# Narrow products padded to the full array, and scan levels issued in three groups, in a two-block transformer kernel

## The chip, the cores and the metric

The kernel runs on one core of a Trainium2 chip, as one program. The metric is the device time of one execution in microseconds (us), the median of three runs. Five engines work in parallel, each through its own list of instructions in order: TensorE (PE, with its weight loads listed as PEld), VectorE (DVE), ScalarE (ACT), GpSimd (POOL) and SyncE (SP), which only starts transfers here. They wait for each other by semaphores.

## The reference

512 tokens of width 1024 pass through two transformer blocks in FP32. The first: half an FFN, a mixed attention (eight heads of block-sparse attention with compressed, selected and window keys, and eight "fox" heads of forgetting attention), half an FFN, a gate. The second: sixteen meta tokens are put ahead, then eight heads of the HGRN2 recurrence beside a convolution, then an FFN with a convolution. What the change touches is, in the reference:

```python
# forgetting attention, a block of 128 queries; c = cumsum(log_f)
logits = (jnp.einsum('bhqd,bhsd->bhqs', qq, k).astype(jnp.float32) * scale
          + cq[..., :, None] - c[:, :, None, :])
p = masked_softmax(logits, kpos[None, :] <= tpos[:, None])
...
# the recurrence S_t = diag(f_t) S_{t-1} + k_t v_t^T, o_t = S_t^T q_t, in chunks
G = jnp.cumsum(gb, axis=-2)
o_inter = jnp.einsum('bhtd,bhdv->bhtv', qb * jnp.exp(G), S)
decay = jnp.exp(jnp.where(causal, G[:, :, :, None, :] - G[:, :, None, :, :], -jnp.inf))
A = jnp.sum(qb[:, :, :, None, :] * kb[:, :, None, :, :] * decay, axis=-1)
o = o_inter + jnp.einsum('bhts,bhsv->bhtv', A, vb)
k_dec = kb * jnp.exp(G[:, :, -1:, :] - G)
S_new = jnp.exp(G[:, :, -1, :])[..., None] * S + jnp.einsum('bhsd,bhsv->bhdv', k_dec, vb)
```

## The kernel before

Activations lie with features on the 128 partitions and tokens along the free dimension. An FP32 product with a weight is three products of rounded parts (`x1h`,`whi`; `x1l`,`whi`; `x1h`,`wlo`, and the same with `x0`): each weight tile `wraw` comes by DMA, ScalarE rounds it to `whi`, VectorE makes the rest `wlo`. Weight projections fill most of TensorE's list; with the two halves of one projection they accumulate in `acc`. Smaller products in plain FP32 run as two passes each, so the trace counts two instructions (`x8` for four products).

The order of the work is written when the program is built. Class `Clocks` keeps a modelled clock for each engine, and `Engine._note` charges each instruction. Small tasks (generators, started with `spawn`) are let in between two weight products by `run` when the planner's clock says that their operands are ready. A task's `yield` is such a place. All instructions are recorded in one helper, so that the profile gives line 144 for all of them and a reader goes by the names of tiles.

Attention. `unit` (L1076) does one head and one block of 128 queries, with 128 to 512 keys. It makes the scores `s` (shown as `b`, a bank of the accumulation memory) from two products of `x1h`/`x1l` parts of q and k. For the fox heads a third product adds the bias: row `extra` of `CC`, which holds the cumulated gates in rows 0 to 7 and their rounding rest in rows 32 to 39, is picked by a column of `selr`, broadcast along the free dimension. Both tiles have 40 rows. Then VectorE takes the minimum, ScalarE the exponential, TensorE transposes `p`, ScalarE copies, TensorE multiplies by `VF`. `ev_aux` (L819) fills `selr` and `CC`.

Recurrence. `hgrn` (L1722) does one of eight heads; while it runs, the main loop goes through the projections of the next. The score matrix of a chunk of 128 tokens is put together from seven levels: at level `hs` the tokens are cut into pairs of blocks of `hs`, `level(hs)` subtracts gates (VectorE), takes exponentials (ScalarE), scales k and q into a tile `wX` (VectorE) and multiplies the two halves. At 64 this is four products of 64 columns, at 32 eight of 32; at 16 to 1, `diag` does 16 of 32 columns for four chunks, and below 16 one of 16x4 for the four last meta tokens, with a mask applied afterwards. The set for the diagonal itself, `diag(5, k, q)`, stands at the start. Each level issues as soon as it is scaled. When all seven are issued, ScalarE copies the blocks of levels 64 and 32 into the matrix `AT`, VectorE masks and sums the small levels (`tmm`, `tm`, `rd`, `am`) and copies `rd` into `AT`, and ScalarE copies the level of 16 in eight pieces. Then TensorE multiplies `am` by `vm` (four queries over the 16 meta tokens) and, per chunk, `AT` by `vt` and the carried state `sv` by `qe`. Squares, `rsqrt`, scaling and transposes (`ident`,`wX`; `ident`,`om`) follow. `carry` (L1912) transposes the decayed keys `kd` and multiplies `kt` by `vt` for three chunks and `km` by `vm` for the meta tokens. `vm` is the fifth part of the tile `vt`, `km` the fourth of `kt`; both have 16 rows, `am` has 16 rows and 4 columns, `om` four rows.

Of the kernel before, what the change touches and what calls it, by code (L numbers as in the profile page):

```python
# [8 lines left out]
FT = mybir.dt.float32  # L9
FR = mybir.dt.float32r  # L10
AF = mybir.ActivationFunctionType
OP = mybir.AluOpType
AX = mybir.AxisListType

SEQ, DM, DFF, META = 512, 1024, 2816, 16
# [3 lines left out]
PRE = 4  # L19
# [6 lines left out]
EPS = 1e-6  # L26
BIG = 1e30
LEVELS = (16, 8, 4, 2, 1)
NS, NZ, NPROB = 10, 3, 8

HALF_GROUPS = {"kk": (768, 1024), "qa0": (0, 128), "cc": (512, 640), "qa1": (256, 384), "vf0": (2328, 2456),
# [260 lines left out]
def build(tc, A, out):  # L292
# [70 lines left out]
    rtok = base.tile([128, 5], FT, name="rtok")  # L363
# [408 lines left out]
    with tc.tile_pool(name="att", bufs=1) as pool:  # L772
# [3 lines left out]
        def kk(name):  # L776
            o, w = KOFF[name]
            return kc[:, o:o + w]

        selr = pool.tile([40, 8], FR, name="selr")  # L780
        CC = pool.tile([40, SEQ], FR, name="CC")
        VF = pool.tile([128, 4, 8, 65], FT, name="VF")
        VS = pool.tile([128, 4, 4, 65], FT, name="VS")
        GF = pool.tile([128, 4, 32], FT, name="GF")
# [33 lines left out]

        def ev_aux(bs):  # L819
            yield lambda: done["rB"]  # L820
            act(selr, kk("sel")[:40], AF.Copy)
            for t in range(4):
                V.tensor_scalar(GF[:, t], bs[t].t[:, 256:288], rtok[:, t:t + 1], None, op0=OP.mult)
                S.activation(VS[:, t, :, 0:64], bs[t].t[:, 0:256].rearrange("p (a d) -> p a d", a=4), AF.Copy,
                             scale=rtok[:, t:t + 1])
                bs[t].free()
                yield
            hs = [sc.get() for _ in range(4)]
            z, e, u, l = (x.t[:8] for x in hs)
            b = yield from banks.take(1)  # L830
            for t in range(4):
                P.transpose(b.t[:8, t * 128:(t + 1) * 128], GF[:, t, 24:32], ident)
            yield
            V.tensor_scalar(z, b.t[:8], pc("b_forget", rows=8), None, op0=OP.add)
            b.free()
            yield

            act(G3, GF[:, :, 0:24], AF.Exp, scale=-1.0)
            S.activation(e, z, AF.Abs)
            act(e, e, AF.Exp, scale=-1.0)  # L840
            yield
            V.tensor_scalar(G3, G3, 1.0, None, op0=OP.add)
            V.reciprocal(G3, G3)
            V.tensor_tensor(G0V, G3.rearrange("p t (h j) -> p t h j", j=3)[:, :, :, 0],
                            kk("vcmp")[:, :, None].to_broadcast([128, 4, 8]), op=OP.mult)

            V.tensor_scalar(u, e, 1.0, None, op0=OP.add)
            yield
            act(l, u, AF.Ln, exact=True)
            V.tensor_scalar(u, u, -1.0, None, op0=OP.add)  # L850
            V.tensor_sub(e, e, u)
            V.tensor_scalar(z, z, 0.0, None, op0=OP.min)
            V.memset(u, 1.0)
            yield
            V.tensor_add(l, l, e)
            V.tensor_sub(z, z, l)
            yield
            V.tensor_tensor_scan(l, u, z, 0.0, op0=OP.mult, op1=OP.add)
            S.activation(CC, causal[:40], AF.Copy, scale=0.0)
            yield  # L860
            S.activation(CC[0:8], l, AF.Copy)
            yield
            V.tensor_sub(CC[32:40], l, CC[0:8].bitcast(FT))
            for x in hs:
                x.free()
            done["aux"] = True
# [212 lines left out]
        def unit(u, hp):  # L1079
            q, k, qt, extra = u["q"], u["k"], u["qt"], u["head"]  # L1080
            n = (qt + 1) * 128
            p = hp.t
            lq = q[:, qt * 128:qt * 128 + 128]
            yield seen(lq, k[0][:, :n], k[1][:, :n])
            s = yield from banks.take(1)
            P.matmul(s.t[:, :n], lq, k[0][:, :n], start=True, stop=False)
            P.matmul(s.t[:, :n], lq, k[1][:, :n], start=False, stop=extra is None)
            if extra is not None:

                P.matmul(s.t[:, :n], selr[:, extra:extra + 1].to_broadcast([40, 128]), CC[:, :n],  # L1090
                         start=False, stop=True)
            for f_ in u["free"]:
                f_()
            yield
            mn = pool.tile([128, 1], FT, name="mn", bufs=8)
            V.tensor_tensor_reduce(out=p[:, :n], in0=s.t[:, :n], in1=causal[:, 512 - n:], scale=1.0,
                                   scalar=3e38, op0=OP.add, op1=OP.min, accum_out=mn)
            s.free()
            yield
            act(p[:, :n], p[:, :n], AF.Exp, scale=-1.0, bias=mn)  # L1100
            yield
            hpt = yield from sc.take()
            t = yield from banks.take(1)
            for kb in range(qt + 1):
                P.transpose(t.t[:, kb * 128:kb * 128 + 128], p[:, kb * 128:kb * 128 + 128], ident)
            hp.free()
            flying["n"] -= 1
            yield
            S.activation(hpt.t[:, :n], t.t[:, :n], AF.Copy)
            t.free()  # L1110
            yield u["ready"]
            o = yield from banks.take(1)
            for kb in range(qt + 1):
                P.matmul(o.t[:, :65], hpt.t[:, kb * 128:kb * 128 + 128], u["v"](kb), start=kb == 0, stop=kb == qt)
            hpt.free()
            yield
            rc = pool.tile([128, 1], FT, name="rc", bufs=8)
            V.reciprocal(rc, o.t[:, 64:65])
            u["fin"](o.t, rc)
            o.free()  # L1120
            u["after"]()
# [454 lines left out]
    with tc.tile_pool(name="hgrn", bufs=1) as pool:  # L1576
# [4 lines left out]
        lb = pool.tile([128, 8], FT, name="lb")  # L1581
        lb1 = pool.tile([128, 8], FT, name="lb1")
        rB2 = pool.tile([128, TC], FT, name="rB2")
        ATs = []
        for i in range(2):
            t = pool.tile([128, 4, 128], FT, name=f"AT{i}")
# [6 lines left out]
        for n_, c_ in (("q", 2), ("f", 1), ("i", 1), ("g", 2), ("a", 1), ("gb", 1), ("cv", 1), ("yb", 2), ("k", 1),  # L1593
                       ("G", 1), ("eg", 1), ("X", 4), ("qe", 1), ("os", 1)):
            stores[n_] = Store(pool, "w" + n_, c_, [128, TN if n_ in ("g", "a", "gb", "cv", "yb", "os") else T2])
        stores["vt"] = Store(pool, "vt", 1, [128, 5, 128])
        stores["kt"] = Store(pool, "kt", 1, [128, 4, 128])
        stores["sv"] = Store(pool, "sv", 1, [128, 4, 128])
        done = {"rB": False, "mixed": 0, "last": False}

# [124 lines left out]
        def hgrn(st):  # L1725
# [8 lines left out]
            V.tensor_scalar(k, f, -1.0, 1.0, op0=OP.mult, op1=OP.add)  # L1734

            hvt = yield from stores["vt"].take()
            vt, vm = hvt.t, hvt.t[:META, 4]
            pv = yield from banks.take()
            for c in range(4):
                P.transpose(pv.t[:, c * 128:(c + 1) * 128], ctile(zi, c), ident)  # L1740
# [9 lines left out]
            V.tensor_tensor_scan(gc, reset, f, 0.0, op0=OP.mult, op1=OP.add)  # L1750
            st["f"].free()
            yield
            S.activation(vm, pv.t[:META, :128], AF.Copy, scale=rtok[:META, 4:5])
            pv.free()
            he = yield from stores["eg"].take()
            eg = he.t
            act(eg, gc, AF.Exp)
            state = {"n": 0, "sv": None}
            px = yield from banks.take()
            pd = []  # L1760
            for _ in range(2):
# [17 lines left out]
            def level(hs):  # L1779
# [11 lines left out]
                V.tensor_mul(xb[:, :, 0], xb[:, :, 0], kb_[:, :, 0])  # L1791
                V.tensor_mul(xb[:, :, 1], xb[:, :, 1], qb[:, :, 1])
                yield
                if hs == 64:
                    for c in range(4):
                        o_ = META + 128 * c
# [13 lines left out]

            for hs in (64, 32, 16, 8, 4, 2, 1):
                spawn(level(hs))
            diag(5, k, q)
            yield lambda: state["n"] == 7
            st["q"].free()
            hk.free()
# [1 line left out]
            at = ATs[cb % 2]  # L1818
            rd = pool.tile([128, 4, 32], FT, name="rd")
            tmm = pool.tile([META, 5, PRE], FT, name="tmm")  # L1820
            am = pool.tile([META, PRE], FT, name="am")
            dn = px.t[:, :384].rearrange("p (c t) -> p c t", c=4)
            S.activation(at[0:64, :, 64:128], dn[0:64, :, 0:64], AF.Copy)
            S.activation(at[0:32, :, 32:64], dn[0:32, :, 64:96], AF.Copy)
            S.activation(at[64:96, :, 96:128], dn[64:96, :, 64:96], AF.Copy)
            V.tensor_tensor(tmm, md, mD[:META, 1:, CUT:META], op=OP.mult)
            V.tensor_reduce(out=am, in_=tmm.rearrange("p l t -> p t l"), op=OP.add, axis=AX.X)
            for i in range(2):
                tm = pool.tile([128, 2, 5, 32], FT, name="tm")
                pi = pd[i].t[:, :384].rearrange("p (c l t) -> p c l t", c=2, l=6)  # L1830
# [18 lines left out]
            for _ in range(2):  # L1849
                po.append((yield from banks.take()))  # L1850
            done["last"] = cb == KB - 1
            om = po[1].t[:PRE, :128]
            P.matmul(om, am, vm, start=True, stop=True)
            for c in range(4):
                d = po[0].t[:, c * 128:c * 128 + 128]
# [11 lines left out]
            for c in range(4):  # L1867
                S.activation(sq[:, c * 128:c * 128 + 128], po[0].t[:, c * 128:c * 128 + 128], AF.Square,
                             accum_out=t_[:, c:c + 1])
            S.activation(sq[:PRE, :128], om, AF.Square, accum_out=t_[:PRE, 4:5])  # L1870
            yield
            V.tensor_scalar(v_, t_, 1.0 / 128, EPS, op0=OP.mult, op1=OP.add)
            yield from rsqrt(r_, v_, t_)
# [1 line left out]
            for c in range(4):  # L1875
                S.activation(sq[:, c * 128:c * 128 + 128], po[0].t[:, c * 128:c * 128 + 128], AF.Copy,
                             scale=r_[:, c:c + 1])
            om_ = pool.tile([PRE, 128], FT, name="om", bufs=2)
            V.tensor_scalar(om_, om, r_[:PRE, 4:5], None, op0=OP.mult)
            yield  # L1880
            for c in range(4):
                P.transpose(po[0].t[:, c * 128:c * 128 + 128], sq[:, c * 128:c * 128 + 128], ident)
            P.transpose(po[1].t[:, 128:128 + PRE], om_, ident[:PRE, :PRE])
            hx.free()
            yield
            ho = yield from stores["os"].take()
# [17 lines left out]
        def carry(st, hk, hg, he, hvt, state):  # L1904
# [14 lines left out]
            V.tensor_mul(kd, kd, k)  # L1919
            yield  # L1920
            hkt = yield from stores["kt"].take()
            kt, km = hkt.t[:, :3], hkt.t[:META, 3]
            pk = yield from banks.take()
            for c in range(3):
                P.transpose(pk.t[:, c * 128:(c + 1) * 128], ctile(kd, c), ident)
# [1 line left out]
            hx.free()  # L1927
            yield
            S.activation(kt, pk.t[:, :384].rearrange("p (c t) -> p c t", c=3), AF.Copy)
            S.activation(km, pk.t[:META, 384:512], AF.Copy)  # L1930
            yield
            su = pk.t
            P.matmul(su[:, 0:128], km, vt[:META, 4], start=True, stop=True)
            for c in range(3):
                P.matmul(su[:, (c + 1) * 128:(c + 2) * 128], kt[:, c], vt[:, c], start=True, stop=True)
            hkt.free()
# [315 lines left out]
```

## Time and profile before

| | |
|---|---|
| median of three runs | 2038.01 us (2037.46 to 2038.76) |
| profiled execution | 2039.5 us, its span 2037.7 us |
| TensorE busy | 99%, 14058 instructions |
| VectorE, ScalarE, GpSimd busy | 59%, 43%, 0% |
| TensorE's granted clock | full in all 40 slices |
| attention's stretch with bias products | 589 to 656 us |
| recurrence | from 1123 us on, its last head's products until 1610 us |

How to read it: durations of products overlap, since a product starts while the one before it drains; so the cost of one on TensorE is the difference of two starts in the timeline. A count `x102` stands for neighbours with the same names and form. A bracket at the end of a row is idle time of that engine before it, with what ended it.

### The profile page before, as it was taken

Reading aid. Unit: us, or ns where it says so; the run is one execution under the profiler, and the core shown is the slowest. Engines: PE = TensorE matmul, PEld = TensorE weight load, DVE = VectorE, ACT = ScalarE, POOL = GpSimd, SP = SyncE. Lnnn points to the kernel's source line nnn. Section 1 sums busy time; section 2 is a strip of 40 time slices with the busy share of each in tenths; the row PEclk is TensorE's granted clock in tenths of the full one; section 3 lists DMA queues with packets and bytes.
Section 4 is the critical chain, followed back from the end, with each engine's and each line's share of the span. In section 5 each row is a group of like instructions: output and inputs, shape, how many; then the busy total and the mean of one; then the engine's idle time right before and its main releaser. Section 6 shows DMA issues by size and latency. Waiting matters only on the chain.

```text
span 2037.7 us, 33936 instructions
## 1 busy us (share of the span) xinstructions
PE 2025.4 (99%) x14058; PEld 1807.2 (89%) x14058; DVE 1209.1 (59%) x2243; ACT 878.7 (43%) x1513; POOL 6.4 (0%) x17
## 2 busy tenths in 40 slices
PE   9999999999999999999999999999999999999998
PEld 7888888999997888888888999999999999888987
DVE  6433444678874854344459567676667766535654
ACT  5322223467767533222345544545545543222223
POOL 0000000000000000000000000000000000000000
PEclk9999999999999999999999999999999999999999
DMA  5223323332000432333233223222222233233222
GB/s 181 93 85 112 102 79 95 110 120 67 27 17 12 135 95 80 102 107 104 71 115 93 91 74 91 67 84 82 75 74 80 68 104 94 74 109 99 91 79 77
DMA packets 58170, 179.16 MB, mean 88 GB/s; under 512 B 7424, under 2 KB 9728, under 8 KB 58016
## 3 DMA queue, kind: packets, MB, share of 16 engines
q1 hardware_dynamic: 57648, 175.56, 28.3%
q8 instruction: 111, 1.82, 0.4%
q0 software_dynamic: 368, 1.42, 0.2%
q14 instruction: 43, 0.35, 0.1%
HBM read 174.86 MB, written 2.10 MB: 87 GB/s over the span
## 4 chain that ended last, share of the span: by engine, by line
PE 98%; DVE 1%; ACT 1%; DMA 0%; issue 0%; SPq 0%; DVEq 0%
PE b L144 57%; PE acc L144 29%; PE h L144 12%; DMA wraw<-in_ffn_wu 0%; DVE h L144 0%; ACT x1h L144 0%; ACT x1l L144 0%; DVE x1h L144 0%; ACT AT L144 0%; DVE s L144 0%; DVE rd L144 0%; ACT L144 0%; ACT whi L144 0%; ACT s L144 0%; DVE OA L144 0%
## 5 line engine op out<-in xcount | busy, mean ns | idle before, releaser
L144 DVE TENSOR_TENSOR wlo<-wraw,whi 128x1024 fp32r<-128x1024 f32 (+4 forms) x365 | 402.6, 1104 | 321.6 <-ACT whi L144 316.8
L144 ACT ACTIVATE whi<-wraw 128x1024 fp32r<-128x1024 f32 (+4 forms) x364 | 348.0, 961 | 423.1 <-PE h L144 138.8
L144 PE MATMUL acc<-x1h,whi 128*128 128x258 f32 (+2 forms) x1472 | 305.0, 288 | 0.0
L144 PE MATMUL acc<-x1h,wlo 128*128 128x258 f32 (+2 forms) x1472 | 296.8, 283 | 0.0
L144 PE MATMUL acc<-x1l,whi 128*128 128x258 f32 (+2 forms) x1472 | 296.6, 283 | 0.0
L144 PEld LDWEIGHTS acc<-x1h,whi 128*128 128x128 f32 x1472 | 228.5, 189 | 3.8
L144 PEld LDWEIGHTS acc<-x1h,wlo 128*128 128x128 f32 x1472 | 227.8, 189 | 0.0
L144 PEld LDWEIGHTS acc<-x1l,whi 128*128 128x128 f32 x1472 | 227.8, 189 | 0.0
L144 PE MATMUL b<-x0h,whi 128*128 128x512 f32 (+2 forms) x504 | 193.4, 386 | 1.2 <-ACT whi L144 0.9
L144 PE MATMUL b<-x0l,whi 128*128 128x512 f32 (+2 forms) x504 | 192.3, 384 | 0.0
L144 PE MATMUL b<-x0h,wlo 128*128 128x512 f32 (+2 forms) x504 | 192.2, 384 | 0.1
L144 PE MATMUL b<-x1h,whi 128*128 128x512 f32 (+1 forms) x368 | 140.4, 385 | 0.0
L144 PE MATMUL b<-x1h,wlo 128*128 128x512 f32 (+1 forms) x368 | 140.2, 385 | 0.0
L144 PE MATMUL b<-x1l,whi 128*128 128x512 f32 (+1 forms) x368 | 140.2, 384 | 0.0
L144 PE MATMUL b<-hh,whi 128*128 128x512 f32 x352 | 136.9, 389 | 0.0
L144 PE MATMUL b<-hl,whi 128*128 128x512 f32 x352 | 136.9, 389 | 0.0
L144 PE MATMUL b<-hh,wlo 128*128 128x512 f32 x352 | 136.9, 389 | 0.0
L144 ACT ACTIVATE hh<-u 128x512 fp32r<-128x512 f32 x66 | 41.7, 632 | 169.4 <-DVE u L144 169.4
L144 PEld LDWEIGHTS b<-x0h,whi 128*128 128x128 f32 x504 | 94.6, 189 | 20.5 <-ACT whi L144 1.2
L144 PEld LDWEIGHTS b<-x0h,wlo 128*128 128x128 f32 x504 | 94.6, 189 | 19.4 <-DVE wlo L144 0.8
L144 PEld LDWEIGHTS b<-x0l,whi 128*128 128x128 f32 x504 | 94.6, 189 | 18.8 <-DVE x0l L144 0.7
L144 PE MATMUL b<-whi,x0h 128*128 128x256 f32 (+1 forms) x352 | 102.3, 291 | 0.3 <-DVE x1h L144 0.3
(371 smaller groups left out, 3550.2 us busy)
## 6 DMA issues: line engine op xcount, KB each, us to landing
wraw<-in_w_in SPq DMA_DIRECT2D x72, 512.0 KB, 3.6
wraw<-in_w_up SPq DMA_DIRECT2D x44, 512.0 KB, 3.6
wraw<-in_ffn_wg SPq DMA_DIRECT2D x43, 512.0 KB, 3.5
wraw<-in_ffn_wu SPq DMA_DIRECT2D x43, 512.0 KB, 3.5
wraw<-in_ffn_wd SPq DMA_DIRECT2D x32, 384.0 KB, 3.1
wraw<-in_ffn_wd SPq DMA_DIRECT2D x32, 320.0 KB, 2.9
wraw<-in_w_half SPq DMA_DIRECT2D x20, 512.0 KB, 3.6
wraw<-in_w_down SPq DMA_DIRECT2D x16, 384.0 KB, 3.1
```

Of the source, the lines that this page charges most:

```text
L144: r = f(*a, **k)
```

## The change

Three things. First, `selr` and `CC` get 128 rows in place of 40; the rows that carry nothing are zero. Second, `vm`, `km`, `am` and `om` become four tiles of 128x128 that are zeroed once by GpSimd; the 16- and 4-row parts are written as before, and the products and the transpose take the whole tiles. Third, a level that has been scaled waits until every level of its group has been, `GROUPS`, and the set for the diagonal moves from the start of the head to the level of 16.

```diff
+GROUPS = ((64, 32), (16, 8), (4, 2, 1))
...
-        selr = pool.tile([40, 8], FR, name="selr")
-        CC = pool.tile([40, SEQ], FR, name="CC")
+        selr = pool.tile([128, 8], FR, name="selr")
+        CC = pool.tile([128, SEQ], FR, name="CC")
...
-            act(selr, kk("sel")[:40], AF.Copy)
+            act(selr, kk("sel"), AF.Copy)
...
-            S.activation(CC, causal[:40], AF.Copy, scale=0.0)
+            S.activation(CC, causal, AF.Copy, scale=0.0)
...
-                P.matmul(s.t[:, :n], selr[:, extra:extra + 1].to_broadcast([40, 128]), CC[:, :n],
+                P.matmul(s.t[:, :n], selr[:, extra:extra + 1].to_broadcast([128, 128]), CC[:, :n],
...
+        vm, km, am = (pool.tile([128, 128], FT, name=n_) for n_ in ("vm", "km", "am"))
+        om_ = pool.tile([128, 128], FT, name="om")
+        for t in (vm, km, am, om_):
+            G.memset(t, 0.0)
...
-        stores["vt"] = Store(pool, "vt", 1, [128, 5, 128])
-        stores["kt"] = Store(pool, "kt", 1, [128, 4, 128])
+        stores["vt"] = Store(pool, "vt", 1, [128, 4, 128])
+        stores["kt"] = Store(pool, "kt", 1, [128, 3, 128])
...
-            state = {"n": 0, "sv": None}
+            state = {"n": 0, "sv": None, "scaled": set()}
...
+                state["scaled"].add(hs)
+                group = next(g for g in GROUPS if hs in g)
+                yield lambda: all(i in state["scaled"] for i in group)
+                if hs == 16:
+                    diag(5, k, q)
...
-            diag(5, k, q)
             yield lambda: state["n"] == 7
...
-            V.tensor_reduce(out=am, in_=tmm.rearrange("p l t -> p t l"), op=OP.add, axis=AX.X)
+            V.tensor_reduce(out=am[:META, :PRE], in_=tmm.rearrange("p l t -> p t l"), op=OP.add, axis=AX.X)
...
-            om = po[1].t[:PRE, :128]
+            om = po[1].t[:, :128]
             P.matmul(om, am, vm, start=True, stop=True)
...
-            P.transpose(po[1].t[:, 128:128 + PRE], om_, ident[:PRE, :PRE])
+            P.transpose(po[1].t[:, 128:256], om_, ident)
...
-            P.matmul(su[:, 0:128], km, vt[:META, 4], start=True, stop=True)
+            P.matmul(su[:, 0:128], km, vm, start=True, stop=True)
```

The planner writes TensorE's list anew. The rows below are its list for the head with index 2, from its last small levels to the products of `AT`; `wX` with a number is the tile of one level, `acc` rows are the projections of the next head. First the list before, where two levels stand together and nine rows of projections lie between them and the last two:

```order
L144 MATMUL b_11882<-wX_12038 32x32 x8
L144 MATMUL b_11883<-wX_12038 32x32 x8
L144 MATMUL b_11881<-wX_12038 16x4
L144 MATMUL acc_12107<-x1h,whi 128x264 x2
...
L144 MATMUL b_11881<-wX_12041 16x4
L144 MATMUL b_11882<-wX_12074 32x32 x8
L144 MATMUL b_11883<-wX_12074 32x32 x8
L144 MATMUL b_11881<-wX_12074 16x4
L144 MATMUL acc_12208<-x1h,whi 128x264 x2
...
L144 MATMUL b_12324<-vt_11763,am 4x128
L144 MATMUL b_12323<-vt_11763,AT_9757 128x128
L144 MATMUL b_12323<-sv_12114,wqe_11930 128x128
```

Between the last level and the product of `am` stand 21 rows of projections, 42 products. The same place in the list now:

```order
L145 MATMUL b_11886<-wX_12015 32x32 x8
L145 MATMUL b_11887<-wX_12015 32x32 x8
L145 MATMUL b_11885<-wX_12015 16x4
L145 MATMUL b_11886<-wX_12024 32x32 x8
L145 MATMUL b_11887<-wX_12024 32x32 x8
L145 MATMUL b_11885<-wX_12024 16x4
L145 MATMUL b_11886<-wX_12187 32x32 x8
L145 MATMUL b_11887<-wX_12187 32x32 x8
L145 MATMUL b_11885<-wX_12187 16x4
...
L145 MATMUL b_12354<-vm,am 128x128
L145 MATMUL b_12353<-vt_11767,AT_9765 128x128
L145 MATMUL b_12353<-sv_12059,wqe_11923 128x128
```

Three levels stand together, and the rows left out are 18 of projections, 36 products; this is so in heads 0 to 5, with 42 in head 6 and 48 in head 7. Over all heads TensorE's list had 41 separate groups of such products and has 24.

On ScalarE the place is the junction of heads 6 and 7. `AT` rows are the copies into head 6's matrix, `wi` is the copy of head 7's values, which TensorE transposes. Before:

```order
L144 ACTIVATE AT_9757<-b_15073 64x4x64
L144 ACTIVATE AT_9757<-b_15073 32x4x32 x2
L144 ACTIVATE AT_9757<-b_15074 16x2x16 x4
L144 ACTIVATE AT_9757<-b_15075 16x2x16 x4
L144 ACT_TABLE_LOAD
L144 ACTIVATE wq_15399<-wq_15399 128x528
L144 ACTIVATE whi<-wraw 128x1024
L144 ACTIVATE wi_15530<-acc_15402 128x528
```

Between the copies and `wi` stand a table load, `wq` and a weight copy. The same place now:

```order
L145 ACT_TABLE_LOAD
L145 ACTIVATE wq_15375<-wq_15375 128x528
L145 ACTIVATE whi<-wraw 128x1024
L145 ACTIVATE AT_9765<-b_15069 64x4x64
L145 ACTIVATE AT_9765<-b_15069 32x4x32 x2
L145 ACTIVATE AT_9765<-b_15070 16x2x16 x4
L145 ACTIVATE AT_9765<-b_15071 16x2x16 x4
L145 ACTIVATE wi_15515<-acc_15378 128x528
```

The three stand ahead of the copies, and `wi` directly behind them. ScalarE's list has 50 table loads where it had 48.

## Rows read from the trace of the kernel before

**Rows 1.** The page: busy us and instructions by engine; the chain that ended last.
```profile
PE 2025.4 (99%) x14058; PEld 1807.2 (89%) x14058; DVE 1209.1 (59%) x2243; ACT 878.7 (43%) x1513; POOL 6.4 (0%) x17
...
PE 98%; DVE 1%; ACT 1%; DMA 0%; issue 0%; SPq 0%; DVEq 0%
```

**Rows 2.** Waits of TensorE: for whom, us in total, times, longest.
```profile
PE b L144 <- ACT wi L144: 0.3, 1, 0.3
```

**Rows 3.** Timeline of TensorE, 631 to 634: start us, us, instruction, tiles, count.
```profile
631.97 0.40 PE L144 MATMUL b<-x1h 128*128 128x512 f32 x1
632.29 0.50 PE L144 MATMUL b<-CC,selr 40*128 40x512 f32 x1
632.72 0.50 PE L144 MATMUL b<-x0h,whi 128*128 128x512 f32 x1
633.06 0.40 PE L144 MATMUL b<-x0l,whi 128*128 128x512 f32 x1
633.29 0.39 PE L144 MATMUL b<-x0h,wlo 128*128 128x512 f32 x1
```

**Rows 4.** Tile CC: ns shortest/median/longest, first and last start, forms.
```profile
L144 PE MATMUL b<-CC,selr x32: 322/410/497, 589.5 to 654.3; 40*128 40x512 f32 x8, 40*128 40x384 f32 x8, 40*128 40x256 f32 x8, 40*128 40x128 f32 x8
```

**Rows 5.** Windows: us, busy of PE, PEld, DVE, ACT, POOL, clock, DMA.
```profile
589.00:630.00 41.00, 40.28 (x264) 32.87 (x264) 28.64 (x94) 36.22 (x83) 0.00 (x0) 1.00 0.04 14
630.00:656.00 26.00, 26.00 (x164) 20.09 (x163) 10.86 (x48) 16.63 (x46) 0.00 (x0) 1.00 0.04 11
```

**Rows 6.** Timeline of TensorE, 605 to 606.
```profile
605.77 0.66 PE L144 MATMUL b<-ident,OA 128*128 128x128 f32 x4 [0.66 <-DVE OA L144]
```

**Rows 7.** Timeline of TensorE, 1597 to 1602, two groups of small products.
```profile
1597.68 0.40 PE L144 MATMUL acc<-x1l,whi 128*128 128x260 f32 x2
1597.92 0.41 PE L144 MATMUL acc<-x1h,wlo 128*128 128x260 f32 x2
1598.26 1.10 PE L144 MATMUL b<-wX 128*32 128x32 f32 x102
1599.29 0.51 PE L144 MATMUL acc<-x1h,whi 128*128 128x258 f32 x2
1599.63 0.40 PE L144 MATMUL acc<-x1l,whi 128*128 128x258 f32 x2
...
1600.93 0.47 PE L144 MATMUL b<-wX 128*32 128x32 f32 x34
1601.33 0.51 PE L144 MATMUL acc<-x1h,whi 128*128 128x258 f32 x2
```

**Rows 8.** Timeline of TensorE, 1178 to 1180, products of the carry.
```profile
1178.14 1.35 PE L144 MATMUL b<-vt,kt 16*128 16x128 f32 x8
1179.24 0.49 PE L144 MATMUL acc<-x1h,whi 128*128 128x264 f32 x2
```

**Rows 9.** Timeline of TensorE, 1199 to 1201, transposes of the head's output.
```profile
1199.45 0.60 PE L144 MATMUL b<-ident,wX 128*128 128x128 f32 x4
1199.98 0.22 PE L144 MATMUL b<-ident,om 4*128 4x4 f32 x1
1200.13 0.50 PE L144 MATMUL acc<-x1h,whi 128*128 128x258 f32 x2
```

**Rows 10.** Timeline of all engines, 1309 to 1317, head 2 up to `AT`'s products.
```profile
1310.34 0.51 PE L144 MATMUL acc<-x1h,whi 128*128 128x264 f32 x2
...
1314.46 1.75 ACT L144 ACTIVATE AT<-b 16x32 f32<-16x32 f32 x8 [3.17 <-DVE AT L144]
...
1315.67 0.38 PE L144 MATMUL b<-vt,am 16*4 16x128 f32 x2
1315.98 0.49 PE L144 MATMUL b<-vt,AT 128*128 128x128 f32 x2
1316.30 0.39 PE L144 MATMUL b<-sv,wqe 128*128 128x128 f32 x2
1316.53 0.39 PE L144 MATMUL b<-vt,AT 128*128 128x128 f32 x2
```

## The prediction made before the changed kernel ran

> **What bounds the kernel now.** I began with the page: engine shares, then the chain of waits. TensorE is busy 99% of the span and the chain that ended last is 98% TensorE [rows 1]. The reader is to see that there is no second bound in the whole: what TensorE saves shortens the time unless a new wait eats it. The view of the waits of TensorE lists eight, one of which, 0.3 us on `wi`, touches this change [rows 2]. So the work is to price, in starts on TensorE, each product that is padded or regrouped, and then to look for the waits that a faster TensorE runs into. Prices are differences of starts in the timeline, since the durations of pipelined products overlap.
>
> **Attention: 40 rows become 128.** A bias product of 512 columns: x1h starts 0.32 before it, it takes 0.43 to the next start, and the one behind it takes 0.34; an undisturbed product of that width takes 0.23 [rows 3]. So one costs 0.09 ahead, 0.19 to 0.20 itself and 0.08 to 0.11 behind. There are 32, eight of each width, from 589.5 to 654.3 [rows 4]. With all 32 read in this way the excess is 32 x 0.09 = 2.9 ahead, 8 x (0.19 + 0.19 + 0.19 + 0.14) = 5.7 itself for 512, 384, 256 and 128 columns, and 32 x 0.08 = 2.6 behind: 11.2 us. Padded, it has the shape of its neighbours, and I take its excess as nothing; bounds: 0 to 11.2 saved, since no row shows a 128-row product with a broadcast stationary operand. I take 11.2, as the operand's load is the only thing left that differs.
>
> What gives some back: ScalarE. From 589 to 630 it is busy 36.2 of 41.0 us [rows 5], half of the bias products lie there, so TensorE would shorten that stretch by 5.6 to 35.4, less than ScalarE's work, and TensorE waits there already 0.66 once for the heads' summed outputs [rows 6]. The pitch of ScalarE's instructions overlaps a little, so its own minimum is below 36.2; I put it at 34 to 36 with gaps, and take 2.3 of the 11.2 as given back (bounds 0 and 5.6, all of that stretch). Attention: 11.2 - 2.3 = 8.9 us. Behind 630 ScalarE has room, 16.6 of 26.0 [rows 5]. The copies into `CC` and `selr` have more partitions and the same columns, so I cost them at nothing; ScalarE's work there is covered by projections on TensorE.
>
> **Recurrence: fewer groups of narrow products.** Three sets of 34 products (102) take 1.03 from their start to the next ordinary start, one set 0.40 [rows 7], so each further set costs (1.03 - 0.40)/2 = 0.315 and a group has 0.40 - 0.315 = 0.085 of its own inside. The product pair ahead of a group takes 0.34, as does the pair behind it, against 0.24 between undisturbed pairs [rows 7]; over many groups that is 0.09 and 0.10. A separate group thus costs 0.275 beyond its products. By the order before has 41 groups (five a head, six in the last), the changed kernel 24: 17 x 0.275 = 4.7 us. Within a new group, the 64-row products stand directly ahead of the 32-row ones, a neighbourhood that no row prices: 0 to 0.275 for each of 8 heads. I take 0.15, the middle: 1.2 us. Groups: 3.5 saved.
>
> The row shows that a change from full to narrow products and back costs 0.275 [rows 7]. The Trainium skill, page "TensorEngine Tiling (Array Packing)", section "Key Properties", has "Changing tiling mode (not just tile) drains the TensorE". By that rule the step from 64 to 32 columns inside a group would cost a whole change again, 8 x 0.275 = 2.2 in place of 1.2, and the forecast would be 1.0 later. The trace agrees for full against narrow; for 64 against 32 nothing here shows it.
>
> **Recurrence: padded products.** `km`/`kt`: four products in eight passes take 1.10 to the next start [rows 8]; eight full passes take 8 x 0.112 = 0.90 (0.23 for two passes on the full array [rows 10]). With 0.09 ahead and 0.10 behind, as at a group, that is 0.39 a head, 3.1 us. The transposed `om`: four full transposes take 0.53 to the start of the small one, which takes 0.15 [rows 9]; a pass takes 0.112, so 0.08 + 0.04, and 0.10 behind: 0.22 a head, 1.8 us. The product `am`: 0.31 to the next start and 0.32 for the pair behind it against 0.224 each [rows 10], with 0.09 ahead 0.276 a head, 2.2 us. Below nothing none of these comes, as the number of passes stays and only the rows grow. Together 3.1 + 1.8 + 2.2 = 7.1; with the groups 10.6 us.
>
> Four zeroings on GpSimd are added where the recurrence's stage begins; that engine is nearly idle, and the first use is a head's projections later: nothing. The stores `vt` and `kt` lose a part nobody else uses: nothing. Two more table loads on ScalarE, which has slack in that stage: nothing; if that cover were gone they would be in the wait priced next.
>
> **What is late next.** The chain from the last scores to the matrix `AT`: last small group ends, ScalarE copies three blocks, VectorE multiplies and reduces, copies four blocks, ScalarE copies eight more. In head 2 the first product behind the last group starts at 1310.34 (T0). ScalarE begins the eight at 1314.46 and takes 1.75 for them, so the first four, which the first product reads, end about 1315.4, T0 + 5.1. TensorE comes to that product at 1315.98, T0 + 5.64 [rows 10]: no wait, 0.5 to spare. In the new order 36 products stand in that place instead of 42, so 6 x 0.12 = 0.72 earlier, and `am` gives up another 0.17: TensorE arrives at about T0 + 4.75, before its operand. The wait is 0.35 to 0.5 in each of heads 0 to 5 (heads 6 and 7 have 42 and 48 products there and room); I take 0.45, in all 2.7 us given back. Bounds: 0, if the levels' scores are ready earlier, as the old chain's 0.5 was no less than this, and 4.5, with the squares and transposes behind it late as well. Behind the waiting product on TensorE's queue stand the eight others of the head and then the projections; VectorE and ScalarE run ahead of those and do not need them at once.
>
> At the junction of heads 6 and 7 TensorE waited 0.33 for `wi` [rows 2], which stood on ScalarE behind a table load, the step on the next `wq` and a weight copy; in the new order it follows the `AT` copies at once. 0.3 us gained; bounds 0 and 0.4.
>
> **Sum.** 8.9 + 10.6 + 0.3 - 2.7 = 17.1 us. The profiled execution took 2039.5 us (span 2037.7), so 2022.4 against it; the median of the three runs is 1.5 lower, 2038.0, so the forecast is 2020.9 us.
>
> **Rivals.** (a) No new waits, everything is paid out: 11.2 + 10.6 + 0.3 = 22.1, 2015.9 us. For it: TensorE has almost no wait now [rows 2], the order is written for it, and ScalarE's overlapped pitch. Against it: the 0.5 of [rows 10] is less than what is taken away in front of it. Chance 0.17. (b) ScalarE sets the pace of the attention stretch: its 36.2 us are the floor, the second half's products follow it as well, and 5 to 9 of the 11.2 are given back instead of 2.3: 2023.5 to 2027.5 us. For it [rows 5, 6], against it the second half, where TensorE has no gap. Chance 0.18. (c) The slower side: each level is held until the last of its group is scaled, so TensorE comes to a group of three with the last one not ready, and the whole chain to `AT` begins later. Its price is one wait a head; it decides from 22.1/8 = 2.8 us a head, about nine times the 0.315 that a set takes and five times the 0.5 to spare. Against it: the order was set by the planner's clock, under which no group of before waits, and the projections around it can be moved. At 2.8 a head the time is that of before, at 4 a head 2048. Chance 0.05, of which 0.02 slower. (d) The slowness in attention belongs to the broadcast operand and not to its 40 rows, so nothing is saved there: 2020.9 + 8.9 = 2029.8. Against it: the cost ahead and behind is like that of the small groups, whose operands are not broadcast [rows 3, 7]. Chance 0.04.
>
> **How the numbers follow.** Forecast 0.56, with its own range of 2017.5 to 2025 (waits of 0 to 4.5, attention's give-back a little over or under, 64 beside 32 columns at 0 or 2.2). With (a) and (b) the range for 8 in 10 is 2015 to 2028. What a measurement of this kernel can tell from no change is about 0.2%, 4 us: faster are the forecast, (a), (b) and (d), 0.95; within it 0.03 and slower 0.02, from (c).
>
> **What would show it.** The bias product of 512 columns at 0.23 to the next start, and none of the 0.09 on either side; if it stays at 0.43, (d). In the windows of attention, the stretch with the first 16 shortened by 3 to 5.6, and idle TensorE with a softmax tile named as releaser; more than 3 idle is (b). In the recurrence three groups a head, ordinary neighbours of `km`, `am` and `om` at 0.11 a pass, and a wait of 0.3 to 0.5 on `AT` in six heads: none of these is (a), one above 2 us is (c). It is wrong if the group of 64 and 32 costs more than 0.3 beyond its products, or if TensorE waits at groups.

## The result, and the profile after

The changed kernel took 2025.6 us (median of 6 runs, 2025.2 to 2027.8) against 2038.0 us (6 runs, 2037.5 to 2039.4): 12.4 us less, a ratio of 0.994 with a 95% interval of 0.9927 to 0.9953. TensorE's granted clock is full in all 40 slices of both profiles, so the clock has no part in it. The forecast was 2020.9 us, 17.1 us less. The measured time lies in the stated range, 0.6 us above the forecast's own range of 2017.5 to 2025, and at a time that rival (b) had priced; whether by (b)'s mechanism is the question below.

From the page of the changed kernel, the busy time by engine and the chain that ended last, as in [rows 1]:

```profile
PE 2007.6 (99%) x14058; PEld 1804.9 (89%) x14058; DVE 1208.4 (60%) x2243; ACT 883.7 (44%) x1515; POOL 7.0 (0%) x21
...
PE 93%; ACT 3%; DVE 2%; issue 1%; DMA 0%; SPq 0%; DVEq 0%; ACTq 0%
```

TensorE lost 17.8 us of busy time, and the span (2024.9 us) fell by 12.8 only. The chain says where the rest is: 5% of it now runs through ScalarE and VectorE, before it was 2%. TensorE's waits, by what released them, with the total, the times and the longest:

```profile
PE b L145 <- ACT AT L145: 2.1, 6, 0.6
...
PE b L145 <- ACT s L145: 0.9, 2, 0.7
PE b L145 <- ACT wX L145: 0.8, 4, 0.2
...
PE b L145 <- ACT VF L145: 0.6, 1, 0.6
...
PE b L145 <- ACT vt L145: 0.3, 1, 0.3
PE b L145 <- ACT OB L145: 0.3, 1, 0.3
```

None of the six was there before. `AT`, `wX` and `vt` belong to the recurrence, `s`, `VF` and `OB` to attention.

To place the loss I subtract the starts of the same instruction in both traces. At the first bias product the changed kernel is already 0.9 us ahead; nothing differs up to there, and in the other kernels of this study that lead is 0.2 to 1.6, so it is the run's start and no effect. The lead is counted from it:

| the same instruction | before, starts at us | after, starts at us | lead us |
|---|---|---|---|
| first bias product | 589.50 | 588.61 | 0 |
| 17th bias product | 632.29 | 629.04 | 2.4 |
| end of attention (`x0l`,`whi`) | 660.20 | 651.39 | 7.9 |
| start of the recurrence (fifth `ident`,`wi`) | 1159.46 | 1150.70 | 7.9 |
| behind the recurrence (`x0h`,`whi`) | 1640.00 | 1627.25 | 11.9 |

So attention saved 7.9 (forecast 8.9), the recurrence with the junction of heads 6 and 7 saved 4.0 (forecast 8.2).

**The padded products cost what was forecast.** TensorE's timeline at the bias product of [rows 3]:

```profile
628.80 0.40 PE L145 MATMUL b<-x1h 128*128 128x512 f32 x1
629.04 0.39 PE L145 MATMUL b<-CC,selr 128*128 128x512 f32 x1
629.27 0.39 PE L145 MATMUL b<-x0h,whi 128*128 128x512 f32 x1
629.50 0.40 PE L145 MATMUL b<-x0l,whi 128*128 128x512 f32 x1
629.73 0.39 PE L145 MATMUL b<-x0h,wlo 128*128 128x512 f32 x1
```

From start to start that is 0.24, 0.23, 0.23, 0.23: nothing is left of the excess, ahead, itself or behind. The windows of the two halves of attention, to be held against [rows 5]:

```profile
588.10:626.50 38.40, 36.54 (x270) 32.85 (x268) 27.81 (x93) 35.40 (x81) 0.00 (x0) 1.00 0.04 15
626.50:647.20 20.70, 20.40 (x161) 19.25 (x160) 10.86 (x50) 16.37 (x46) 0.00 (x0) 1.00 0.05 14
```

In the first half ScalarE is busy 35.4 of 38.4 us and TensorE idles 1.9, most of it in the waits for `s` and `VF`, which ScalarE writes; that for `OB` follows at 627.4. The stretch became 2.6 us shorter (41.0 to 38.4), less than the 3 to 5.6 that the prediction named as its sign. From the first to the 17th bias product the lead grows by 2.4 of the 5.6 that these products gave up, in the second half by 5.5 of 5.6. Attention gives back 3.3 us, nearly all of it ahead of the 17th bias product, where ScalarE has little room.

In the recurrence, the timeline of TensorE in the order of time: at the group of 64 and 32, at the transposes of the output, at `km`/`kt`, and at a group of three levels:

```profile
1163.84 1.05 PE L145 MATMUL b<-wX 128*64 128x64 f32 x24
1164.82 0.66 PE L145 MATMUL b<-ident,wX 128*128 128x128 f32 x4
...
1193.05 0.40 PE L145 MATMUL acc<-x1h,wlo 128*128 128x258 f32 x2
1193.60 0.65 PE L145 MATMUL b<-ident,wX 128*128 128x128 f32 x4
1194.09 0.27 PE L145 MATMUL b<-ident,om 128*128 128x128 f32 x1
1194.12 0.49 PE L145 MATMUL acc<-x1h,whi 128*128 128x258 f32 x2
...
1227.99 0.39 PE L145 MATMUL b<-vm,km 128*128 128x128 f32 x2
1228.21 0.83 PE L145 MATMUL b<-vt,kt 128*128 128x128 f32 x6
1228.80 0.49 PE L145 MATMUL acc<-x1h,whi 128*128 128x258 f32 x2
...
1594.13 0.41 PE L145 MATMUL acc<-x0h,klo 128*128 128x258 f32 x2
1594.46 1.10 PE L145 MATMUL b<-wX 128*32 128x32 f32 x102
1595.50 0.51 PE L145 MATMUL acc<-x0h,khi 128*128 128x258 f32 x2
```

`km`/`kt` take 0.81 instead of the 1.10 of [rows 8]; the group of 102 takes 1.04 as in [rows 7]. The transposes show something else: the two products ahead (1193.05) take 0.55 to the next start instead of 0.24. That is a wait, and the smaller cost of the padded `om` is gone in it.

**Where TensorE waits now.** The timeline of all engines in head 2, answering [rows 10]:

```profile
1304.27 0.51 PE L145 MATMUL acc<-x1h,whi 128*128 128x264 f32 x2
...
1308.40 1.75 ACT L145 ACTIVATE AT<-b 16x32 f32<-16x32 f32 x8 [3.16 <-DVE AT L145]
...
1308.74 0.38 PE L145 MATMUL b<-vm,am 128*128 128x128 f32 x2
1309.39 0.49 PE L145 MATMUL b<-vt,AT 128*128 128x128 f32 x2 [0.27 <-ACT AT L145]
1309.72 0.39 PE L145 MATMUL b<-sv,wqe 128*128 128x128 f32 x2
```

T0 is 1304.27 here, the start of the first product behind the last group. ScalarE begins its eight copies at T0 + 4.13 as before; TensorE is through with the 36 products and `am` at T0 + 4.7 and stands until T0 + 5.12. `am` takes 0.65 to the next start where 0.22 is its own, 0.43 too much, and the pair behind the wait takes 0.33 instead of 0.22. So this wait costs 0.54 by the starts, twice the idle time of 0.27 that the bracket shows: the bracket begins only when `am`'s own duration of 0.38 has ended, and without a wait the next product starts before that. From the first `am` to the first ordinary product the eight heads take 2.71, 2.64, 2.46, 2.47, 2.47, 2.46, 2.36 and 1.92. Heads 6 and 7 have no wait: the 2.36 holds the four transposes of `wi`, 0.44, which now stand directly behind these products. Against 1.92 the first six heads lose 3.7 us.

The second wait is on `wX`, the scaled output, and has a cause that I had not seen. First the kernel before in head 3, all engines, from the first product of `AT` over the copy of the next head's values (`wi`) to the square of `om`:

```profile
1377.36 0.49 PE L144 MATMUL b<-vt,AT 128*128 128x128 f32 x2
...
1377.63 1.06 ACT L144 ACTIVATE whi<-wraw 128x1024 fp32r<-128x1024 f32 x1
...
1378.71 0.61 ACT L144 ACTIVATE wi<-acc 128x528 f32<-128x528 f32 x1
1378.71 1.23 DVE L144 TENSOR_TENSOR wlo<-wraw,whi 128x1024 fp32r<-128x1024 f32 x1 [2.15 <-ACT whi L144]
...
1379.89 0.06 DVE L144 MEMSET hnv<- 128x1 f32 x1
...
1380.52 0.25 ACT L144 ACTIVATE wX<-b 4x128 f32<-4x128 f32 x1
```

And the same place after:

```profile
1370.46 0.49 PE L145 MATMUL b<-vt,AT 128*128 128x128 f32 x2 [0.28 <-ACT AT L145]
...
1371.24 0.61 ACT L145 ACTIVATE wi<-acc 128x528 f32<-128x528 f32 x1
...
1371.75 1.05 ACT L145 ACTIVATE whi<-wraw 128x1024 fp32r<-128x1024 f32 x1
...
1372.83 1.22 DVE L145 TENSOR_TENSOR wlo<-wraw,whi 128x1024 fp32r<-128x1024 f32 x1 [2.65 <-ACT whi L145]
...
1374.01 0.06 DVE L145 MEMSET hnv<- 128x1 f32 x1
...
1374.17 0.27 ACT L145 ACTIVATE wX<-b 4x128 f32<-4x128 f32 x1 [0.34 <-DVE hnv L145]
...
1377.04 0.66 PE L145 MATMUL b<-ident,wX 128*128 128x128 f32 x4 [0.20 <-ACT wX L145]
```

A fill of one column takes 0.06 us, but it stands on VectorE behind a weight's lower half, which waits for ScalarE's upper half. In the new order ScalarE copies `wi` before that upper half, so the upper half comes 1.29 behind the first product of `AT` (1370.46) instead of 0.27 behind it (1377.36), the fill with it, and ScalarE's square of `om`, which writes that column, now waits 0.34 for the fill. TensorE's transposes are late by it. Six heads lose 0.36 to 0.44 there, 2.4 us in all. At the groups themselves the trace has another 0.5: 0.01 to 0.14 above the usual, in six groups of the heads 0, 2, 4 and 6. That TensorE waits at groups was one of the prediction's signs of being wrong; it came, and it is the smallest of the three. 3.7 + 2.4 + 0.5 = 6.6 us given back, against a forecast saving of 7.1 for the padding and 3.5 for the groups; 4.0 is left.

The forecast's 0.3 at the junction of heads 6 and 7 is not there. The four transposes of `wi` no longer wait, but the fifth, of the meta tokens' values, now waits 0.33 for ScalarE at 1561.91: the wait for `vt` in the list above.

### The profile page after: what moved, and what is told of

The parts are those of the page before. It is cut to its first block, busy times and chain, and to the rows that moved or that the text cites. A ratio compares the mean times of both kernels' runs of the same rounds, so it can differ in the third digit from the quotient of the medians.

```text
span 2024.9 us, 33933 instructions
## 1 busy us (share of the span) xinstructions
PE 2007.6 (99%) x14058; PEld 1804.9 (89%) x14058; DVE 1208.4 (60%) x2243; ACT 883.7 (44%) x1515; POOL 7.0 (0%) x21
## 4 chain that ended last, share of the span: by engine, by line
PE 93%; ACT 3%; DVE 2%; issue 1%; DMA 0%; SPq 0%; DVEq 0%; ACTq 0%
PE b L145 56%; PE acc L145 26%; PE h L145 12%; ACT AT L145 1%; DVE rd L145 1%; ACT s L145 0%; DVE wlo L145 0%; ACT wX L145 0%; ACT whi L145 0%; DVE tm L145 0%; ACT x1l L145 0%; ACT x1h L145 0%; DVE AT L145 0%; DMA wraw<-in_ffn_wu 0%; DVE hnv L145 0%
```

## The experiments

The nine timed kernels, each against runs of the kernel before on the same chip. "Recurrence" is the lead gained between its start and its end in the trace, worked out as above from one profiled execution of each kernel, and free of the run's start. The kernel with 64 rows at the end, whose recurrence is that of the changed kernel, repeats the 4.0 of the first row as 4.1.

| kernel | median us | before us | ratio, 95% interval | recurrence us |
|---|---|---|---|---|
| changed | 2025.6 | 2038.0 | 0.9940 (0.9927 to 0.9953) | 4.0 |
| attention padded only | 2030.3 | 2038.6 | 0.9961 (0.9949 to 0.9974) | 0.0 |
| recurrence padded only | 2031.7 | 2038.6 | 0.9968 (0.9956 to 0.9980) | 6.8 |
| groups only | 2039.8 | 2038.6 | 1.0006 (0.9997 to 1.0015) | -0.7 |
| changed, no groups | 2024.0 | 2038.6 | 0.9930 (0.9918 to 0.9943) | 6.6 |
| changed, fill earlier | 2025.3 | 2038.6 | 0.9933 (0.9920 to 0.9947) | 5.9 |
| changed, last products later | 2022.7 | 2038.6 | 0.9925 (0.9913 to 0.9938) | 7.7 |
| changed, both | 2022.6 | 2038.6 | 0.9923 (0.9911 to 0.9936) | 8.4 |
| both, last head ungrouped | 2022.8 | 2038.2 | 0.9923 (0.9909 to 0.9937) | 8.1 |

Intervals of kernels 1 to 2 us apart overlap; what separates those is the trace.

**Attention alone.** The five lines of the diff that pad `selr` and `CC`, and nothing else.

> The kernel before with only CC and selr padded to 128 rows. Theory (the shortfall against the forecast lies in the recurrence's new stalls): the trace of the changed kernel lies 8.0 us ahead at the end of attention, so 8.0 us faster than before, about 2030.0 us, and the order behind attention as before. Rival (attention gives back most of it to ScalarE, the shortfall of 4.6 us lies here): 4.3 us faster at most, 2033.7 us.

8.3 us faster; the trace has 7.9 in attention and none behind it. Of the shortfall against the forecast only 1.0 lies there, and rival (b), which has all of it there, falls.

**Recurrence padded alone.** The change without the lines on `selr`, `CC` and `GROUPS`; `diag(5, k, q)` at the start as before.

> The kernel before with only vm, km, am and om padded; CC, selr and the issue of the levels as before. Theory (the regrouping brings the stalls, the padding is paid out in full): 3.1 + 1.8 + 2.2 = 7.1 us faster than before, about 2030.9 us, with no wait of TensorE on AT and none on the scaled outputs over 0.1 us. Rival (padding makes TensorE early, and the stalls come with it whatever the grouping): 0 to 1 us faster, about 2037.5 us, with the same waits on AT in six heads as in the changed kernel.

6.9 us faster, 6.8 by the trace, and TensorE's waits name neither `AT` nor `wX`. The padding pays 7.1 nearly in full; its stalls, if it had any, would be here. The 0.3 that is missing is at the junction of heads 6 and 7, where TensorE's wait for `wi` is 0.6 in place of 0.3.

**Groups alone.** The kernel before with

```diff
+GROUPS = ((64, 32), (16, 8), (4, 2, 1))
...
-            state = {"n": 0, "sv": None}
+            state = {"n": 0, "sv": None, "scaled": set()}
...
+                state["scaled"].add(hs)
+                group = next(g for g in GROUPS if hs in g)
+                yield lambda: all(i in state["scaled"] for i in group)
+                if hs == 16:
+                    diag(5, k, q)
...
-            diag(5, k, q)
```

> The kernel before with only the three groups of levels and the moved diagonal set; all tiles narrow as before. Theory: the groups save 0.43 x 8 = 3.4 us and 0.3 at the last junction, but the stalls on AT (2.9, less than in the changed kernel since TensorE comes 0.17 later without the padded am), those on the transposes of the outputs (2.4) and at groups (0.5) cost 5.8: 2.1 us slower than before, about 2040.1 us. Rival (the groups pay as forecast): 1 to 3.5 us faster, about 2035 us.

1.2 us slower, an interval of -0.03% to +0.15%: no change that can be told, and not the gain of the rival. In the trace it loses 0.7. TensorE's waits in it:

```profile
PE b L145 <- ACT AT L145: 1.6, 6, 0.4
...
PE b L145 <- ACT wX L145: 1.2, 6, 0.2
```

With narrow tiles throughout, both waits are there. They belong to the grouping. The stalls read from its starts are 2.0 on `AT`, 2.5 on the transposes and 0.2 at groups, 4.7 in all, where I expected 5.8. With the loss of 0.7 that makes the gross gain of the groups and the junction 4.0, where I expected 3.7. So the loss of 2.1 came out too high, mainly for the stalls.

**The change without the groups.** The same lines taken out of the changed kernel.

> The changed kernel without the groups: every level issues when it is scaled and the diagonal set at the start, as before; all padding stays. Theory: 8.0 + 7.1 = 15.1 us faster than before, about 2022.9 us, that is 2.7 us faster than the changed kernel. Rival (the stalls belong to the padding, the groups gain): 2029 us, slower than the changed kernel by 3.4 us.

2024.0 us, 14.6 us less than before where the changed kernel has 12.4. The two ratios' intervals overlap, so the times alone don't rank them; the traces do, 6.6 against 4.0 in the recurrence with the same 7.9 in attention. The third part of the change took back 2.6 us of the other two.

**The fill earlier.** In the changed kernel:

```diff
+            nv = pool.tile([128, 3, 8], FT, name="hnv", bufs=2)
+            v_, r_, t_ = (nv[:, i, :5] for i in range(3))
+            V.memset(t_[:, 4:5], 1.0)
             yield lambda: state["sv"] is not None
...
-            nv = pool.tile([128, 3, 8], FT, name="hnv", bufs=2)
-            v_, r_, t_ = (nv[:, i, :5] for i in range(3))
-            V.memset(t_[:, 4:5], 1.0)
```

> The changed kernel with VectorE's zero-cost fill of one column of hnv issued before the head's last products in place of behind them, where it stood behind a weight's lower half and held up ScalarE's square of om. Theory: the stall of 0.36 to 0.44 us on the transposes of the outputs goes in six heads, 2.4 us, about 2023.2 us; the stalls on AT (4.1 us) stay. Rival (the chain of squares, logarithm and scaling is itself too long for the 36 products in front, with or without the fill): no change, 2025.6 us.

All engines in head 3 of this kernel:

```profile
1371.47 1.23 DVE L145 TENSOR_TENSOR wlo<-wraw,whi 128x1024 fp32r<-128x1024 f32 x1 [2.52 <-ACT whi L145]
...
1372.34 0.25 ACT L145 ACTIVATE wX<-b 4x128 f32<-4x128 f32 x1
...
1375.32 0.60 PE L145 MATMUL b<-ident,wX 128*128 128x128 f32 x4
```

Counted from the products of `AT`, the weight's lower half is where it was; the square of `om` no longer waits, and neither do the transposes: the bracket is gone in heads 0 to 5. The recurrence gains 1.9 of the 2.4 expected; in head 6 the transposes now lose 0.2, and in the output projection of the last head TensorE idles 0.3 which cost 0.8 by the starts. The time, 13.3 less than before, is too close to the changed kernel's 12.4 to show it. So, by the trace, the fill held up this chain; the chain itself is short enough.

**The last products later.** In the changed kernel, `at` being the matrix and `M` the planner's clock:

```diff
+            ripe = M.written(at) + 700.0
-            yield lambda: state["sv"] is not None
+            yield lambda: state["sv"] is not None and M.now() >= ripe
```

> The changed kernel with the head's last products told to start 0.7 us later by the planner's clock, which puts 42 products of the next projections in front of them in place of 36 in heads 0 to 5. Theory: the stalls on AT go (4.1 us, up to 0.3 us left in heads 0 and 1), and since the products then end 0.25 us later against the fill on VectorE, part of the stall on the transposes as well: 4 to 6 us faster than the changed kernel, 2019.5 to 2021.6 us. Rival (what follows AT is bound by ScalarE's and VectorE's chain, so that the wait only moves to the transposes): 2024 to 2025.6 us.

42 products stand there instead of 36, `AT` is no longer among TensorE's waits, and the recurrence gains 3.7. (Head 6 still takes 2.36 from `am` on: the 4.1 of the two expectations counts its four transposes as a wait.) At the transposes 0.24 to 0.36 a head stays, 1.7 in six heads. 2022.7 us, 1 us above what I expected.

**Both.**

> Both of these edits. Theory: no stall left in the recurrence above 0.2 us, 6.6 us faster than the changed kernel, about 2019.0 us, 19 us faster than before. Rival: 2023 to 2024 us, with waits of the same sum on other tiles.

TensorE's timeline of this kernel, head 3 at `AT`, and the end of the last head:

```profile
1366.95 0.38 PE L145 MATMUL b<-vm,am 128*128 128x128 f32 x2
1367.16 0.39 PE L145 MATMUL b<-vt,AT 128*128 128x128 f32 x2
...
1605.84 0.51 PE L145 MATMUL acc<-x0h,khi 128*128 128x258 f32 x2 [0.81 <-ACT x0h L145]
1606.57 0.51 PE L145 MATMUL acc<-x0l,khi 128*128 128x258 f32 x2 [0.22 <-DVE x0l L145]
```

`am` takes its 0.21, and no head waits at `AT` or at the transposes. Its time is the lowest, level with the kernel ahead of it and the next one, but 16.0 us less than before, not 19: nearer to the rival's 2023 to 2024 than to the 2019.0 of the theory, and as the rival has it, a wait has moved to other tiles. The recurrence has 8.4 of the 10.9 that the padding, the groups and the junction were to save. More than half of the rest is in these last rows: TensorE has come to the output projection of the last head before that head's output exists. It idles 1.0 there, 1.5 by the starts, where the changed kernel did not wait.

**The last head ungrouped.** I took this for an effect of the groups in the last head.

```diff
-                group = next(g for g in GROUPS if hs in g)
+                group = next(g for g in GROUPS if hs in g) if cb < KB - 1 else (hs,)
```

and `diag(5, k, q)` at the start in that head.

> The kernel with both of the edits before (the fill issued earlier, the head's last products 0.7 us later), with the three groups in heads 0 to 6 only; in the last head each level issues by itself and the diagonal set at the start, as in the kernel before. Theory (grouping makes the last head's matrix late, behind which no projections are left to cover its chain, and TensorE waits for the last output there): the trace with both edits lost 2.2 us between the last head's projections and the end of the recurrence; most of that comes back, 1.5 to 2.2 us against it, about 2020.7 us, 18 us faster than before. Rival (that loss is the tail's chain itself, which comes earlier on TensorE's clock whatever the grouping): no change, 2022.6 us.

No change: 2022.8 us, 8.1 in the recurrence. My theory fell. The waits moved: TensorE now stands 0.50 for a VectorE result (`wyb`) ahead of the last head's products. That the tail is bound by the last head's own chain fits both, but no kernel here shortens that chain, so it stays open.

**64 rows.** The changed kernel with `CC` and `selr` of 64 rows, run once.

> The changed kernel with CC and selr of 64 rows in place of 128 (40 before). Read from starts alone. Theory (a product that does not use all rows of the array stands by itself, whatever the count): a bias product of 512 columns takes about 0.43 us to the next start and 0.09 ahead, as with 40 rows. Rival (40 is slow because it is no half or quarter of the array): 0.23 us as with 128.

```profile
630.88 0.40 PE L145 MATMUL b<-x1h 128*128 128x512 f32 x1
631.21 0.50 PE L145 MATMUL b<-CC,selr 64*128 64x512 f32 x1
631.63 0.50 PE L145 MATMUL b<-x0h,whi 128*128 128x512 f32 x1
631.97 0.40 PE L145 MATMUL b<-x0l,whi 128*128 128x512 f32 x1
```

0.33 ahead, 0.42 itself, 0.34 behind: as with 40 rows, and so in all four widths. By the starts attention saves nothing (0.0 us), and the one run took 2034.6. The cost of this product is the same at 40 and at 64 rows; other counts were not run for it.

## Why the prediction was right in direction and 4.7 us short

- The prices of the products held. The bias products went to the pitch of their neighbours (11.2 gross, of which the second half paid out 5.5 of 5.6); rival (d) is excluded, the operand is still broadcast. `km`/`kt` took 0.81, where eight full passes had been put at 0.90. The padding of the recurrence measured 6.8 to 6.9 against 7.1. Inside the group of 64 and 32 columns (1163.84), the last 64-column product takes 0.152 to the next start where 0.058 is usual, and the first two of 32 take 0.052 where the pairs behind them take 0.032: the change costs 0.11 us a head, and 0.15 was taken. By the Trainium skill ("TensorEngine Tiling (Array Packing)", "Key Properties") each change of mode drains the array. The trace agrees that this one costs, at less than half of the 0.275 for the change from full to narrow products and back.
- Attention's give-back was 3.3 instead of 2.3, in the first half as placed. That it is ScalarE's rests on the releasers of the waits there; no run with a faster ScalarE tests it.
- The step that failed is "What is late next". It put 2.7 us for all new waits of the recurrence, and 6.6 was measured. At `AT` the mechanism was right and the size nearly so, 3.7 for 2.7: in head 2 the next start is 0.43 late, as taken (0.45), but I left out the 0.11 that the pair behind the wait costs and the longer waits of heads 0 and 1 (0.79 and 0.72 by the starts). What failed is the overlap behind it: I put the transposes only into the upper bound, of 4.5, since VectorE and ScalarE were to run ahead, and 2.4 came from the fill there. That needed VectorE's and ScalarE's lists at this place, in which `wi` and the weight's upper half had changed places. The waits at groups, 0.5, were put at nothing.
- The junction of heads 6 and 7 was put at 0.3 and gave nothing: the wait moved from the first transposes of `wi` to the last. With 1.0 in attention and 3.9 in the recurrence's waits that is 5.2 less than forecast by the trace, and 4.7 by the medians.
- Rival (a), no new wait, is out by 9.7 us. Rival (b) named the right time for the wrong place: attention alone is 8.3 us faster. The forecast's own range ended at 2025; that 2025.6 lies in the stated range is luck to this extent, as the upper part of that range was there for (b). Rival (c) is nearest to what was seen: holding the levels back does cost TensorE waits in every head but the last. The wait that it names, at a group whose last level is not scaled, is 0.5 us in all; with `AT` and the transposes it is 6.6 us, 0.8 a head, where 2.8 would have decided the sign. Alone, the groups cost all that they gain.

## What to carry to other kernels

A regrouping that takes instructions out of the bounding engine's list also takes away the cover in front of the next product that depends on another engine: price the saving and the lost cover in the same row, per head, and price a wait by the starts, not by its idle time (here 0.54 for 0.27). Then follow every instruction on the two other engines between the last input and that product, the small ones too: a fill of 0.06 us cost 0.4 a head because of what stood before it in its queue. Where the parts of a change can be told apart, run them apart; here two of the three are worth more than all three, by the trace (6.6 against 4.0 in the recurrence).

## What the runs showed of the hardware that I had not expected

A product on 64 of 128 rows is no cheaper among full ones than one on 40: 0.42 us to the next start for 512 columns, against 0.43 with 40 rows and 0.23 with 128, and 0.1 more on each side. Padding with zeros to 128 rows is the cheaper form here, in all four widths.
